# Turning k, q and v by VectorE blocks and DRAM in the mixer, and decays from running sums

## The chip, the cores and the metric

The kernel runs on one core of a Trainium2 chip. Its time is device microseconds of one execution; three runs are shown for the kernel before. Beside them stands one profiled execution, from which all durations below come. PE is TensorE, DVE is VectorE, ACT is ScalarE, POOL is GpSimd, and SP is the engine that issues most of the DMAs.

## The reference

One layer of a hybrid decoder trunk in float32, with 256 positions and a width of 2048:

```python
h = rmsnorm(x, norm_mix_w)
q, k, v, z, b_raw, a_raw, p_in, g_a, g_b = split(h @ w_in)
q, k, v = split(silu(causal_dwconv(concat(q, k, v), conv_qkv_w)))     # 4 taps along the sequence
q, k = l2norm per head (16 heads of 128); beta = sigmoid(b_raw)
g = -exp(a_log) * softplus(a_raw + dt_bias)                            # log decay per position and head
# gated delta rule in chunks of 64: cumsum of g in the chunk, decay[i, j] = exp(g_i - g_j) for j <= i,
# a unit lower triangular solve, attention inside the chunk, a state carried from chunk to chunk
y_a = rmsnorm(o) * silu(z)
y_b = (trailing means of p_in - p_in) @ pool_w * pool_scale
x = x + (sigmoid(g_a) * y_a + sigmoid(g_b) * y_b) @ w_out
h = rmsnorm(x, norm_ffn_w); gate, up = split(h @ w_up)
x = x + (gelu(causal_dwconv(gate) + bias) * up) @ w_down
return rmsnorm(x)
```

## The kernel before

**Weights.** Every weight matrix is streamed once, in chunks of 256 rows by 512 columns (512 KB, `raw`, four buffers, loaded by SP in L110). ACT rounds a chunk to the fast fp32 format (`whi`, L112), DVE makes the rest (`wlo`, L119); both have three buffers. PE then does three products in place of one (L149, L150, L151): 12 matmuls of 128x512 for a chunk. Chunks are begun two ahead of the one in use (`AHEAD`).

**Stages.** The mixer works through four groups g of four heads. Each group is a row of gemms: k, q, v, the pooling's input, the gate g_b, the pooling's own product, z and the gate g_a, nearly all of eight chunks. The output projection, the FFN (22 gemms of eight chunks) and the last projection follow. The output projection is begun before group 3 of the mixer is finished.

**Work beside the gemms.** A gemm's result lies in PSUM with positions on the partitions. `evict` (ACT, L422) copies it out. The convolution wants channels on the partitions, so `conv_silu` (L425) calls `turned` (L167), which has PE transpose the 128x128 blocks into PSUM (L175): eight for each of k, q and v. ACT starts the convolution (L436), DVE adds three taps (L439), and the tanh form of silu ends in `kq` or `vT` (L443). The list `later` holds such work until the second chunk of the following gemm. The solve of a group, `gdn` (L445), is a generator, advanced once for each half chunk (`side`). It first makes the decays: DVE scales a triangular matrix by the log decays in two parts (r0, r1; L464, L465), PE sums them with `lowr` and `onesr` (L472, L473, L475), ACT exponentiates (L476, L477, L480), POOL clears the part above the diagonal (L482). Later it has PE turn v back to positions on partitions (L553), and ACT scales that into `vt` (L555).

In the FFN the same need is met by `flip` (L155): DVE transposes all 32x32 blocks of an evicted tile in one instruction (L158), four DMAs write the blocks to their places in DRAM (L162), and one reads the turned tile back (L164).

**Order.** A scheduler places each engine's instructions in one fixed sequence when the kernel is built; on the chip each engine takes them strictly in that order and waits on semaphores. DMAs are queued on the engine that issues them, nearly all on SP.

## Time and profile before

| | us |
|---|---|
| runs, median (lowest to highest) | 1582.16 (1582.14 to 1584.18) |
| profiled execution | 1581.35 |
| its span on the core | 1579.6 |
| PE busy | 1556.7 (99% of the span) |
| DVE busy | 1040.2 (66%) |
| ACT busy | 745.8 (47%) |
| POOL busy | 89.4 (6%) |
| mean granted clock | 0.997 |

The span is what the profiler saw on the core; the time is measured around it. A row of a group names line, engine, operation, tiles (written <- read), shapes and count, then busy time and mean ns of one, then the idle time just before with what ended it. A row of waits names who waited at which line for whom, then total us, number and longest. A row of the stage table gives the window, its length, PE's busy time and count, the granted clock, DMA's share and GB/s. A timeline row gives start and duration in us, then engine, line and operation. DMAs are listed with KB each and median us from issue to landing. Matmuls overlap, so their durations add up to more than their share of time.

### The profile page before, as it was taken

To read this page: it belongs to the slowest core of one execution; us is meant where nothing else is said; L and a number is where in the kernel's file an instruction comes from. 1 tells how busy PE (TensorE), PEld (TensorE's weight loads), DVE (VectorE), ACT (ScalarE), POOL (GpSimd) and SP (SyncE) were. 2 spreads that over 40 slices of the span, in tenths; PEclk is the share of its full clock that TensorE was granted. 3 is DMA by queue.
4 is the path that set the end of the run, shared out by engine and by line. 5 is a ranking of instruction groups with operands and counts; after the bars stand their busy time and mean duration, and the time that the engine had idled before them with its cause. 6 is when DMAs were issued, how large, how long until landed. Compare 5 with 4: busy or idle time off the path is not lost.

```text
span 1579.6 us, 20017 instructions
## 1 busy us (share of the span) xinstructions
PE 1556.7 (99%) x7408; PEld 1284.3 (81%) x7408; DVE 1040.2 (66%) x1544; ACT 745.8 (47%) x925; POOL 89.4 (6%) x121
## 2 busy tenths in 40 slices
PE   8999999999999999999999999999999999999997
PEld 6878888888888888787888888888788878888885
DVE  5778757786678757795655666665666666444445
ACT  6545436444545435454454455444454445434344
POOL 3020100100010100102000000000000000000000
PEclk9999999999999999999999999999999999999998
DMA  7656656665556655565555878788777787755553
GB/s 253 181 155 195 193 148 173 167 197 173 155 153 190 197 149 175 164 191 176 198 188 187 238 224 243 242 244 247 232 234 251 230 246 234 239 196 191 196 191 132
DMA packets 263736, 314.61 MB, mean 199 GB/s; under 512 B 109894, under 2 KB 124246, under 8 KB 263510
## 3 DMA queue, kind: packets, MB, share of 16 engines
q1 hardware_dynamic: 260928, 308.85, 64.5%
q10 hardware_dynamic: 2710, 4.48, 0.8%
q8 instruction: 58, 0.95, 0.2%
q14 instruction: 40, 0.33, 0.1%
HBM read 298.61 MB, written 14.68 MB: 198 GB/s over the span
## 4 chain that ended last, share of the span: by engine, by line
PE 86%; DMA 4%; DVE 4%; issue 3%; SPq 1%; POOL 1%; ACT 0%; DVEq 0%; POOLq 0%
PE psm L151 22%; PE psm L150 21%; PE psm L149 21%; PE psg L840 3%; PE psm L839 3%; PE psg L839 2%; PE psm L838 2%; PE psg L838 2%; PE psm L840 2%; DVE wlo L119 2%; DMA gs<-flip 1%; SPq L162 1%; PE psg L491 1%; DMA flip<-tn 1%; PE psg L175 1%
## 5 line engine op out<-in xcount | busy, mean ns | idle before, releaser
L119 DVE TENSOR_TENSOR wlo<-raw,whi 128x1024 fp32r<-128x1024 f32 x528 | 648.5, 1233 | 376.1 <-ACT whi L112 368.6
L112 ACT CAST whi<-raw 128x1024 fp32r<-128x1024 f32 x530 | 556.9, 1053 | 716.2 <-PE psm L150 548.2
L151 PE MATMUL psm<-wlo,xhl 128*128 128x512 f32 x896 | 353.1, 394 | 2.1 <-DVE wlo L119 2.1
L149 PE MATMUL psm<-whi,xhl 128*128 128x512 f32 x896 | 352.3, 393 | 1.3 <-ACT xhl L219 1.3
L150 PE MATMUL psm<-whi,xhl 128*128 128x512 f32 x896 | 351.9, 393 | 0.0
L151 PE MATMUL psm<-wlo,fhl 128*128 128x512 f32 x704 | 273.7, 390 | 1.9 <-DVE wlo L119 1.4
L150 PE MATMUL psm<-whi,fhl 128*128 128x512 f32 x704 | 274.0, 389 | 0.0
L149 PE MATMUL psm<-whi,fhl 128*128 128x512 f32 x704 | 273.9, 389 | 0.0
L151 PEld LDWEIGHTS psm<-wlo,xhl 128*128 128x128 f32 x896 | 168.6, 188 | 37.8 <-DVE wlo L119 3.7
L149 PEld LDWEIGHTS psm<-whi,xhl 128*128 128x128 f32 x896 | 168.7, 188 | 35.4 <-ACT xhl L219 1.7
L150 PEld LDWEIGHTS psm<-whi,xhl 128*128 128x128 f32 x896 | 168.7, 188 | 34.7
L151 PEld LDWEIGHTS psm<-wlo,fhl 128*128 128x128 f32 x704 | 132.1, 188 | 32.0 <-DVE wlo L119 4.8
L150 PEld LDWEIGHTS psm<-whi,fhl 128*128 128x128 f32 x704 | 132.2, 188 | 27.6
L149 PEld LDWEIGHTS psm<-whi,fhl 128*128 128x128 f32 x704 | 132.2, 188 | 27.1
L838 PE MATMUL psg<-whi,hhi 128*128 128x512 f32 x176 | 68.5, 389 | 0.0
L838 PE MATMUL psm<-whi,hhi 128*128 128x512 f32 x176 | 68.5, 389 | 0.0
L839 PE MATMUL psm<-whi,hlo 128*128 128x512 f32 x176 | 68.5, 389 | 0.0
L839 PE MATMUL psg<-whi,hlo 128*128 128x512 f32 x176 | 68.5, 389 | 0.0
L840 PE MATMUL psm<-wlo,hhi 128*128 128x512 f32 x176 | 68.5, 389 | 0.0
L840 PE MATMUL psg<-wlo,hhi 128*128 128x512 f32 x176 | 61.1, 389 | 0.0
L439 DVE SCALAR_TENSOR_TENSOR cy<-psg,cqw,cy 128x255 f32<-128x255 f32 (+1 forms) x144 | 60.5, 473 | 0.4 <-ACT cy L436 0.4
L151 PE MATMUL psm<-wlo,mhi 128*128 128x512 f32 x128 | 50.0, 391 | 0.3 <-DVE wlo L119 0.3
(223 smaller groups left out, 1351.7 us busy)
## 6 DMA issues: line engine op xcount, KB each, us to landing
raw<-in_w_in_dram SPq DMA_DIRECT2D x226, 512.0 KB, 3.9
raw<-in_w_up_dram SPq DMA_DIRECT2D x176, 512.0 KB, 4.5
raw<-in_w_down_dram SPq DMA_DIRECT2D x88, 512.0 KB, 4.5
raw<-in_w_out_dram SPq DMA_DIRECT2D x32, 512.0 KB, 3.5
flip<-tn SPq DMA_DIRECT2D x88, 128.0 KB, 4.7
gs<-flip SPq DMA_DIRECT2D x22, 512.0 KB, 4.7
raw<-in_pool_w_dram SPq DMA_DIRECT2D x8, 512.0 KB, 4.1
x<-in_x_dram SPq DMA_DIRECT2D x4, 512.0 KB, 6.9
```

The source lines that it names most:

```text
L112: nc.scalar.copy(hi, raw)
L119: nc.vector.tensor_tensor(lo, raw, hi.bitcast(F32), op=ALU.subtract)
L149: mm(ps[:, t, :], lh(k, t), hi[:, kk, :], start=(k == 0), stop=False)
L150: mm(ps[:, t, :], ll(k, t), hi[:, kk, :], start=False, stop=False)
L151: mm(ps[:, t, :], lh(k, t), lo[:, kk, :], start=False, stop=(k == nk - 1))
L162: nc.sync.dma_start(dv[a], b[32 * a : 32 * a + 32].rearrange("p t (f j) -> p t f j", j=32))
L175: nc.tensor.transpose(pt[:, ff, t * P : (t + 1) * P], src[:, t, f * P : (f + 1) * P], ident)
L439: nc.vector.scalar_tensor_tensor(y[:, f, s:], gs[:, : S - s], w(j), y[:, f, s:], op0=ALU.mult, op1=ALU.add)
L491: mm(pg0, kq[:, h, 0, 0:P], kq[:, h, :, :], start=True, stop=True)
L838: mm(acc[c][t], lh(k, t), hi[:, kk, :], start=(k == 0), stop=False)
L839: mm(acc[c][t], ll(k, t), hi[:, kk, :], start=False, stop=False)
L840: mm(acc[c][t], lh(k, t), lo[:, kk, :], start=False, stop=(k == KF - 1))
```

## The change

- The evicted k, q and v go through `flip` (with its target as an argument now) instead of PE, straight into `kq` and `vT`; `conv_silu` reads them from there. Its DVE transpose writes into the convolution's own buffers (tag cy).
- After silu, v goes back through a new `flip_back`: one DVE transpose, four DMAs to DRAM, one back into `vt`, where ACT scales it in place.
- The decays no longer use scaled triangles. Once, PE makes running sums of the log decays in each chunk, written to DRAM as rows (`rund`), and six shifts for each position and head. For a group the rows are read back, broadcast to all partitions; POOL puts -1e30 above the diagonal, and ACT takes 24 exponentials of 128x64, each with its shift as bias.

In the diff below, lines in plain words stand for longer pieces that are only removed or are small set-up.

```diff
-    def flip(pool, src, tag, bufs):
-        b = pool.tile([P, 2, 512], F32, tag="tn", name=nm("tn"))
+    def flip(pool, tag, bufs, src, dst):
+        b = pool.tile([P, 2, 512], F32, tag=tag, bufs=bufs, name=nm("tn"))
         nc.vector.transpose(b.rearrange("p t f -> p (t f)"), src.rearrange("p t f -> p (t f)"))
         d = dpool.tile([512, S], F32, tag="flip", name=nm("flip"))
         dv = d.rearrange("(f i) (t a j) -> a i t f j", i=32, t=2, j=32)
         for a in range(4):
             nc.sync.dma_start(dv[a], b[32 * a : 32 * a + 32].rearrange("p t (f j) -> p t f j", j=32))
-        o = pool.tile([P, 4, S], F32, tag=tag, bufs=bufs, name=nm(tag))
-        nc.sync.dma_start(o, d.rearrange("(f p) s -> p f s", p=P))
-        return o
+        nc.sync.dma_start(dst, d.rearrange("(f p) s -> p f s", p=P))
+
+    def flip_back(pool, tag, bufs, src, dst):
+        b = pool.tile([P, 4, S], F32, tag=tag, bufs=bufs, name=nm("tb"))
+        nc.vector.transpose(b.rearrange("p h s -> p (h s)"), src.rearrange("p h s -> p (h s)"))
+        d = dpool.tile([S, 512], F32, tag="back", name=nm("back"))
+        dv = d.rearrange("(n i) (h a j) -> a i h n j", i=32, h=4, j=32)
+        for a in range(4):
+            nc.sync.dma_start(dv[a], b[32 * a : 32 * a + 32].rearrange("p h (n j) -> p h n j", j=32))
+        nc.sync.dma_start(dst.rearrange("p t h d -> p t (h d)"), d.rearrange("(t p) c -> p t c", p=P))
...
+    nc.gpsimd.memset(tri[0:64, 64:P], 0.0)
...
-    onesr, lowr, ghi, glo, tail
+    ntri, ntail, top
...
+    psr = pg([NH, S])
+    for t in range(2):
+        mm(psr[:, t * P : (t + 1) * P], glog[:, t, :], tri, start=True, stop=True)
+    runs = mp.tile([NH, S], F32, name="runs")
+    nc.vector.tensor_copy(runs, psr)
+    rund = dpool.tile([NH, S], F32, tag="rund", bufs=1, name="rund")
+    nc.sync.dma_start(rund, runs)
+    pse = pg([P, 6, NH])
+    for n, mat in ((0, ntri), (2, ntail)):
+        mm(pse[:, n : n + 2, :], mat, glog, start=True, stop=True)
+    mm(pse[:, 4, :], low, glog[:, 0, :], start=True, stop=True)
+    mm(pse[:, 5, :], low, glog[:, 0, :], start=True, stop=False)
+    mm(pse[:, 5, :], top, glog[:, 1, :], start=False, stop=True)
+    shift = mp.tile([P, 6, NH], F32, name="shift")
+    nc.vector.tensor_copy(shift, pse)
...
-    def conv_silu(e, kind, g, dst):
-        pts = turned(e)
+    def conv_silu(kind, g, dst):
...
-            gs = pts[f // 2][:, f % 2, :]
+            gs = dst[:, f, :]
...
-    (gdn: per pair of heads 8 scalings of tri, 6 matmuls, 4 exponentials from PSUM, 2 selects)
+        nc.sync.dma_start(dec0, rund[4 * g : 4 * g + 4, :].partition_broadcast(P))
+        yield
+        for d, src in ((dec1, dec0[:, :, P:S]), (dec0[:, :, 0:P], dec0[:, :, 0:P])):
+            nc.gpsimd.affine_select(d, src, pattern=[[0, 4], [1, P]], compare_op=ALU.is_ge, fill=-1e30, base=0,
+                                    channel_multiplier=-1)
+        yield
+        for h in range(4):
+            hh = 4 * g + h
+            for d, n in ((dec0[:, h, 0:64], 0), (dec0[:, h, 64:P], 2), (dec0[:, h, P : P + 64], 4),
+                         (dec0[:, h, P + 64 : S], 5), (dec1[:, h, 0:64], 1), (dec1[:, h, 64:P], 3)):
+                nc.scalar.activation(d, d, AF.Exp, bias=shift[:, n, hh : hh + 1])
+            if h % 2:
+                yield
...
         for h in range(4):
             yield
-            pvt = pg([P, 2, P])
             for t in range(2):
-                nc.tensor.transpose(pvt[:, t, :], vT[:, h, t * P : (t + 1) * P], ident)
-            for t in range(2):
-                nc.scalar.activation(vt[:, t, h, :], pvt[:, t, :], AF.Copy, scale=nk[:, t, h : h + 1])
+                nc.scalar.activation(vt[:, t, h, :], vt[:, t, h, :], AF.Copy, scale=nk[:, t, h : h + 1])
...
             ps = ps_k0 if kind == 1 and g == 0 else gemm_a(xh, xl, KD)
-            e = evict(ps)
-            later.append(lambda e=e, kind=kind, g=g, dst=dst: conv_silu(e, kind, g, dst))
+            flip(mp, "cy", 2, evict(ps), dst)
+            later.append(lambda kind=kind, g=g, dst=dst: conv_silu(kind, g, dst))
+            if kind == 2:
+                later.append(lambda vT=vT, vt=vt: flip_back(mp, "cy", 2, vT, vt))
...
```

The kernel has 85 more DMAs, all on SP: five for each of 12 turns and four turns back, four broadcasts and one write. The scheduler gives new orders. Three places follow; in the rows "waits" names the semaphores (DMAHW a DMA's), and numbers behind a name tell buffers apart.

ACT, group 1, from q's convolution on, where decays are made. Before (L436 convolution, L476, L477 and L480 exponentials, L442 tanh, L112 casts):

```order
L436 ACTIVATE cy_385_2306<-psg_383_2296,cqw_338 128x256 [waits PE_49]
L436 ACTIVATE cy_385_2306<-psg_384_2301,cqw_338 128x256 [waits PE_49]
L476 ACTIVATE dec0_396_2344<-psg_402_2364 128x2x128 [waits PE_49]
L477 ACTIVATE dec1_397_2345<-psg_404_2366 128x256 [waits PE_49]
L112 CAST whi_416_2426<-raw_415_2424 128x1024 [waits DMAHW1_49,DVE_49,PE_49]
L436 ACTIVATE cy_385_2306<-psg_383_2296,cqw_338 128x256 [waits DVE_49]
L436 ACTIVATE cy_385_2306<-psg_384_2301,cqw_338 128x256 [waits DVE_49]
L112 CAST whi_425_2458<-raw_424_2456 128x1024 [waits DMAHW2_49,PE_49,Activation_49]
L480 ACTIVATE dec0_396_2344<-psg_403_2365,tail_490 128x128 [waits PE_49]
L480 ACTIVATE dec0_396_2344<-psg_403_2365,tail_490 128x128
L476 ACTIVATE dec0_396_2344<-psg_412_2409 128x2x128 [waits PE_49]
L112 CAST whi_428_2484<-raw_427_2482 128x1024 [waits DMAHW3_49,PE_49,Activation_49]
```

The changed kernel there:

```order
L112 CAST whi_374_2304<-raw_373_2302 128x1024 [waits DMAHW2_49,DVE_49,PE_49]
L477 ACTIVATE dec0_381_2319<-dec0_381_2319,shift_502 128x64 [waits DMAHW4_49,DVE_49,Pool_49]
L477 ACTIVATE dec0_381_2319<-dec0_381_2319,shift_502 128x64
L477 ACTIVATE dec1_382_2320<-dec1_382_2320,shift_502 128x64 x2
L477 ACTIVATE dec0_381_2319<-dec0_381_2319,shift_502 128x64 x2
L477 ACTIVATE dec1_382_2320<-dec1_382_2320,shift_502 128x64 x2
L477 ACTIVATE dec0_381_2319<-dec0_381_2319,shift_502 128x64 x2
L477 ACTIVATE dec1_382_2320<-dec1_382_2320,shift_502 128x64
L477 ACTIVATE dec0_381_2319<-dec0_381_2319,shift_502 128x64 [waits Pool_49]
L477 ACTIVATE dec0_381_2319<-dec0_381_2319,shift_502 128x64 x5
L112 CAST whi_384_2336<-raw_383_2334 128x1024 [waits DMAHW3_49,DVE_49,PE_49]
L477 ACTIVATE dec1_382_2320<-dec1_382_2320,shift_502 128x64
```

The exponentials of a group now come in two long bursts between casts and wait for the rows' DMA and for POOL, not for PE; the convolution comes later.

ACT, group 1, after v's convolution. Before (L555 scales v, turned back by PE, into `vt`; L689 rounds the pooling's tile, L422 evicts):

```order
L112 CAST whi_493_2882<-raw_492_2880 128x1024 [waits DMAHW0_49,PE_49]
L112 CAST whi_497_2905<-raw_496_2903 128x1024 [waits DMAHW5_49,PE_49,Activation_49]
L112 CAST whi_503_2931<-raw_502_2929 128x1024 [waits DMAHW6_49,DVE_49,PE_49]
L555 ACTIVATE vt_392_2340<-psg_480_2827,nk_394_2342 128x128 [waits PE_49,Pool_49]
L555 ACTIVATE vt_392_2340<-psg_480_2827,nk_394_2342 128x128
L555 ACTIVATE vt_392_2340<-psg_488_2850,nk_394_2342 128x128 [waits PE_49]
L555 ACTIVATE vt_392_2340<-psg_488_2850,nk_394_2342 128x128
L555 ACTIVATE vt_392_2340<-psg_489_2861,nk_394_2342 128x128 [waits PE_49,Pool_49]
L555 ACTIVATE vt_392_2340<-psg_489_2861,nk_394_2342 128x128
L689 CAST phi_482_2835<-psg_490_2866 128x512 [waits PE_49]
L112 CAST whi_512_2999<-raw_511_2997 128x1024 [waits DMAHW7_49,DVE_49,PE_49]
L689 CAST phi_482_2835<-psg_491_2873 128x512 [waits PE_49]
```

The changed kernel (L436 evicts, L684 rounds the pooling's tile, L547 scales `vt`):

```order
L112 CAST whi_449_2760<-raw_448_2758 128x1024 [waits DMAHW3_49,PE_49]
L112 CAST whi_458_2795<-raw_457_2793 128x1024 [waits DMAHW4_49,PE_49,Activation_49]
L436 ACTIVATE ev_453_2787<-psm_420_2540,rs_51_371 128x512 [waits PE_49]
L436 ACTIVATE ev_453_2787<-psm_420_2540,rs_51_371 128x512
L112 CAST whi_463_2831<-raw_462_2829 128x1024 [waits DMAHW5_49,DVE_49,PE_49]
L112 CAST whi_466_2851<-raw_465_2849 128x1024 [waits DMAHW6_49,DVE_49,PE_49]
L684 CAST phi_454_2790<-psg_460_2815 128x512 [waits PE_49]
L547 ACTIVATE vt_306_1916<-vt_306_1916,nk_379_2317 128x128 [waits DMAHW5_49,Pool_49]
L547 ACTIVATE vt_306_1916<-vt_306_1916,nk_379_2317 128x128 x3
L547 ACTIVATE vt_306_1916<-vt_306_1916,nk_379_2317 128x128 [waits Pool_49]
L547 ACTIVATE vt_306_1916<-vt_306_1916,nk_379_2317 128x128 x3
L684 CAST phi_454_2790<-psg_461_2822 128x512 [waits PE_49]
```

The eight scalings wait for the DMA that brings v back, and they stand between the two halves of the pooling's tile, with the cast behind them.

SP, the gemms of k and q of group 1. Before, there are only weight loads (L110); now the turn (L162 to DRAM, L163 back) and the decays' broadcast (L467) stand among them:

```order
L110 DMA raw_349_2162<-in_w_in_dram 128x2x512 [waits DMAHW3_49,DVE_49]
L110 DMA raw_352_2180<-in_w_in_dram 128x2x512 [waits DMAHW4_49,DVE_49]
L162 DMA flip_336_2081<-tn_335_2079 64x16x32 [waits DVE_49]
L162 DMA flip_336_2081<-tn_335_2079 64x16x32 x3
L110 DMA raw_355_2198<-in_w_in_dram 128x2x512 [waits DMAHW5_49,DVE_49]
L110 DMA raw_358_2216<-in_w_in_dram 128x2x512 [waits DMAHW6_49,DVE_49]
L110 DMA raw_361_2234<-in_w_in_dram 128x2x512 [waits DMAHW7_49,DVE_49]
L163 DMA kq_304_1914<-flip_336_2081 128x4x256 [waits DMAHW2_49,DMAHW3_49,DMAHW1_49,DMAHW4_49,DMAHW0_49,PE_49]
L110 DMA raw_368_2264<-in_w_in_dram 128x2x512 [waits DVE_49]
L110 DMA raw_373_2302<-in_w_in_dram 128x2x512 [waits DMAHW5_49,DVE_49]
L110 DMA raw_383_2334<-in_w_in_dram 128x2x512 [waits DMAHW6_49,DVE_49]
```

The load of `kq` waits for PE as well, which has to be done with the group before; the weight loads behind it wait with it.

At the end of the mixer PE has 24 matmuls of the output projection between group 3's last product of the solve (L628) and the transposes of the gated result (L183); before there were 44 between L636 and L175.

More of the change, by code (lines that the diff above doesn't have):

```diff
@@ L291 @@
     nc.vector.tensor_scalar(rsq, rs1, 0.25, None, op0=ALU.mult)
+    low = mp.tile([P, P], F32, name="low")
+    nc.gpsimd.affine_select(low, ones, pattern=[[-1, P]], compare_op=ALU.is_gt, fill=0.0, base=0,
+                            channel_multiplier=1)
     tri = mp.tile([P, P], F32, name="tri")
@@ L296 @@
                             channel_multiplier=-1)
-    low = mp.tile([P, P], F32, name="low")
-    nc.gpsimd.affine_select(low, ones, pattern=[[-1, P]], compare_op=ALU.is_gt, fill=0.0, base=0,
-                            channel_multiplier=1)
-    onesr = mp.tile([P, P], F32R, name="onesr")
-    nc.vector.tensor_copy(onesr, ones)
-    lowr = mp.tile([P, P], F32R, name="lowr")
-    nc.vector.tensor_copy(lowr, low)
+    nc.gpsimd.memset(tri[0:64, 64:P], 0.0)
+    ntri = mp.tile([P, P], F32, name="ntri")
+    nc.gpsimd.tensor_scalar(ntri, tri, -1.0, None, op0=ALU.mult)
+    ntail = mp.tile([P, P], F32, name="ntail")
+    nc.gpsimd.tensor_copy(ntail, ntri)
+    nc.gpsimd.tensor_copy(ntail[0:64, 0:64], low[0:64, 0:64])
+    top = mp.tile([P, P], F32, name="top")
+    nc.gpsimd.memset(top, 0.0)
+    nc.gpsimd.memset(top[0:64], 1.0)
     def same_block(b, name, tag):
@@ L662 @@
         vT = mp.tile([P, 4, S], F32, tag="vT", bufs=1, name=nm("vT"))
+        vt = mp.tile([P, 2, 4, P], F32, tag="vt", name=nm("vt"))
         for kind, dst in ((1, kq[:, :, 0, :]), (0, kq[:, :, 1, :]), (2, vT)):
@@ L788, in features @@
             nc.scalar.activation(e[:, t, :], ps[:, t, :], AF.Copy, scale=rs2[:, t : t + 1])
-        return flip(fp, e, "gs", 2)
+        o = fp.tile([P, 4, S], F32, tag="gs", bufs=2, name=nm("gs"))
+        flip(fp, "tn", 1, e, o)
+        return o
     hhi = []
```

46 lines of the change are left out of this document (4 added, 42 removed).

## The prediction

> **What bounds the kernel now.** I read the page first (busy times, the chain), then PE's waits, then the stage table, then timelines at the places that the change edits.
>
> ```profile
> span 1579.6 us, 20017 instructions
> PE 1556.7 (99%) x7408; PEld 1284.3 (81%) x7408; DVE 1040.2 (66%) x1544; ACT 745.8 (47%) x925; POOL 89.4 (6%) x121
> PE 86%; DMA 4%; DVE 4%; issue 3%; SPq 1%; POOL 1%; ACT 0%; DVEq 0%; POOLq 0%
> PE psg L206 <- DMA nmrows<-in_norm_mix_w_dram: 4.6, 1, 4.6
> PE psm L151 <- DVE wlo L119: 3.7, 8, 0.9
> 100.00:745.00 645.00, 642.21 (x3322) 1.00 0.60 174
> 846.00:1330.00 484.00, 482.12 (x2124) 1.00 0.78 235
> ```
>
> PE is busy 99% of the span and 86% of the chain; after the start it waits for weights for 3.7 us in all. In the mixer (100 to 745 us, which the change edits) PE idles 645.00 − 642.21 = 2.8 us, in the FFN (846 to 1330) 1.9 us; the granted clock is 1.00 in both. So a PE instruction removed from the mixer is worth its full spacing, and every wait that the change adds is worth its length, less what the prepared weights cover.
>
> That cover is read from the steady rows in the FFN, where each chunk of 12 matmuls needs a cast (whi, ACT) and a subtraction (wlo, DVE):
>
> ```profile
> 1092.31 1.05 ACT L112 CAST whi<-raw 128x1024 fp32r<-128x1024 f32 x1 [1.66 <-PE psm L150]
> 1093.40 1.23 DVE L119 TENSOR_TENSOR wlo<-raw,whi 128x1024 fp32r<-128x1024 f32 x1 [1.50 <-ACT whi L112]
> 1095.03 1.05 ACT L112 CAST whi<-raw 128x1024 fp32r<-128x1024 f32 x1 [1.67 <-PE psm L150]
> ```
>
> A cast starts when PE frees a buffer, three chunks back, and one follows another by 2.72 us. The chunk that needs it starts two chunks (5.44 us) later: the cast (1.05) has 4.4 us to spare. The subtraction ends 2.32 us after the cast's start and is first read two matmuls into the chunk, so it has 5.44 + 0.45 − 2.32 = 3.6 us. ACT idles 1.66 us in each chunk, DVE 1.50. A wait of ACT or DVE ahead of these two reaches PE only beyond 3.6 us.
>
> **What PE loses.**
>
> ```profile
> L175 PE MATMUL psg<-ident,ev 128*128 128x128 f32 x96 | 12.8, 272 | 0.0
> L553 PE MATMUL psg<-ident,vT 128*128 128x128 f32 x32 | 4.8, 272 | 0.0
> L472 PE MATMUL psg<-r,lowr 128*128 128x256 f32 x16 | 4.6, 297 | 0.0
> 292.10 1.03 PE L175 MATMUL psg<-ident,ev 128*128 128x128 f32 x8
> 292.89 0.48 PE L151 MATMUL psm<-wlo,xhl 128*128 128x512 f32 x1
> 293.20 0.39 PE L149 MATMUL psm<-whi,xhl 128*128 128x512 f32 x1
> 86.61 0.28 PE L472 MATMUL psg<-r,lowr 128*128 128x256 f32 x1
> 86.73 0.40 PE L150 MATMUL psm<-whi,xhl 128*128 128x512 f32 x1
> 86.97 0.28 PE L472 MATMUL psg<-r,lowr 128*128 128x256 f32 x1
> ```
>
> Durations overlap, so I count by starts. From 292.10 to 293.20 lie eight transposes and one matmul; a chunk is 12 matmuls in 2.72 us, 0.227 each, so the eight cost 0.87 us, 0.109 each. A decay matmul moves the next start by 86.73 − 86.61 = 0.12. Gone are 96 transposes of k, q, v (10.4 us), the 32 of v back (L553, 3.5 us) and 48 decay matmuls (L472, L473, L475: 5.8 us). Added are seven matmuls for running sums and shifts, once; as plain fp32 each shows as two records, so 14 by at most 0.12, 1.7 us, 0.2 of it in place of the old tail's. The balance is −18.2 us, all of it on the path to the end, since PE hardly idles there.
>
> **What the turn costs elsewhere.** The FFN already does 22 such turns. One of them:
>
> ```profile
> L158 DVE STREAM_TRANSPOSE tn<-fev 128x1024 f32<-128x1024 f32 x22 | 27.3, 1243 | 0.0
> 1089.12 1.25 DVE L158 STREAM_TRANSPOSE tn<-fev 128x1024 f32<-128x1024 f32 x1
> 1090.39 5.01 SPq L162 DMA_DIRECT2D flip<-tn  x4
> 1097.98 0.37 SPq L164 DMA_DIRECT2D gs<-flip  x1
> 1103.79 0.41 DVE L797 TENSOR_SCALAR y<-gs,cfw,vec 128x256 f32<-128x256 f32 x1 [3.73 <-DMA gs<-flip]
> DVE y L797 <- DMA gs<-flip: 23.1, 11, 3.7
> DVE y L806 <- DMA gs<-flip: 31.3, 11, 3.6
> gs<-flip SPq DMA_DIRECT2D x22, 512.0 KB, 4.7
> flip<-tn SPq DMA_DIRECT2D x88, 128.0 KB, 4.7
> raw<-in_w_in_dram SPq DMA_DIRECT2D x226, 512.0 KB, 3.9
> ```
>
> From the transpose's start to the first use are 14.7 us here; a turn whose waits are all at their shortest (transpose 1.25, two transfers of 4.7, issues of 1.3) would take 12. DVE waits 54 us for the 22, up to 3.7 each, and PE loses at most its 1.9 us: 0.09 per turn, because four casts and subtractions stand between transpose and use, and four chunks (10.9 us) plus 3.6 to spare hold 14.5.
>
> DVE's own work stays about even (16 transposes of 1.24 us come, 64 scalings of tri, L464 and L465, go). ACT gets 24 exponentials of 128x64 a group for 8 larger ones. No row has that shape, so I bound one by these:
>
> ```profile
> L362 ACT ACTIVATE uu<-na 128x32 f32<-128x32 f32 x1 | 0.2, 219 | 0.0
> L480 ACT ACTIVATE dec<-psg,tail 128x128 f32<-128x128 f32 x16 | 5.0, 363 | 0.0
> 310.82 1.66 ACT L555 ACTIVATE vt<-psg,nk 128x128 f32<-128x128 f32 x6
> ```
>
> Between 219 and 363 ns; nearest by size is the first, and I take 250: 24 are 6.0 us (5.3 to 8.7), to be fitted into idle time of 1.66 a chunk. That is off PE's path by itself and matters where it meets a wait.
>
> The new waits, place by place in the new order; each is reckoned by hand with a landing of 12 us, and the range has 14.7:
> - **k of groups 1 to 3.** Only three subtractions stand between transpose and use. SP's load of the turned tile also has to wait until PE has read the old q for its norm (L633), in the q gemm's third chunk, and three weight loads and the decays' broadcast are queued behind it on SP. From that read on PE has about 9.0 us of prepared work; load 4.7, the four scalings and the subtraction behind eight convolution steps take 10.4. 1.4 each, I take 1.5: 4.5 us.
> - **q of groups 1 to 3.** DVE reaches the transpose 5.5 us after the gemm's end, behind the last multiplications of the group before, instead of the 2.1 of an FFN turn; and two bursts of exponentials stand between the casts. 1.7 each: 5 us.
> - **v, four times**: an FFN turn, 0.3 each: 1 us.
> - **v back, four times.** ACT's eight scalings of vt (0.27 each by the six in 1.66, 2.2 us) wait for the DMA, and every cast behind waits with them. From the tanh's end: 1.3 us to the transpose, 12 of landing, 2.2 of scalings and 0.6 for the pooling's copy give 16.1; the next cast is due 11.5 after it: 4.6 to 6 late (one subtraction can stand in between), less 3.6: 1.0 to 2.4. Between the transpose itself and the scalings stand only three casts. I take the upper end, 2.3 each, since DVE is busier here than in the FFN: 9 us.
> - **Group 0's decays.** Running sums to DRAM (one transfer), broadcast back (another), two selects on POOL, 24 exponentials, all between two casts, and started behind q's convolution: 5 us (0 if the sums are early, 8 by the 14.7).
> - **End of the mixer.** Today the last norm is covered:
>
> ```profile
> 766.31 0.60 ACT L646 ACTIVATE o<-psg 128x512 f32<-128x512 f32 x1 [2.98 <-PE psg L636]
> 767.90 1.64 POOL L651 TENSOR_TENSOR ro<-ro,epsx 128x8 f32<-128x8 f32 x1 [43.41 <-DVE ro L650]
> 774.13 1.23 DVE L717 TENSOR_TENSOR sz<-sz,yb 128x1024 f32<-128x1024 f32 x1
> 776.13 1.03 PE L175 MATMUL psg<-ident,sz 128*128 128x128 f32 x8
> ```
>
>   From 766.31 to 775.36 are 9.0 us, and PE has 44 matmuls (10.0 us) ahead of the transposes. In the new order group 3's solve ends some seven chunks later, and 24 matmuls (5.4 us) are left: 9.0 − 5.4 = 3.6, less a subtraction that moves out of the chain in part: 3 us.
>
> Together 27.5 us. The same hand reckoning gives 0.4 us for an FFN turn where the rows have 0.09, so I take 0.25 off each of 16 turns: 23.5. Of the mixer's 2.8 us of old idle time I let 2 go, since the old places are gone.
>
> Sum: 1581.35 (the profiled execution: span 1579.6 and 1.75 around it) − 18.2 − 2 + 23.5 = 1584.65; the median of the runs shown is 0.8 above the profiled one, so **1585**.
>
> One rule speaks against the change. The Trainium skill (VectorE: DVE Perf Modes, The three transpose paths) gives a 128x128 transpose to TensorE when PSUM is an acceptable target, and says that a plain DMA whose strides do the transposing is 19 times slower than the crossbar's. The trace agrees with the first half in the latency (0.109 us against 12 to 14.7 for a turn) and not with the second here: a turn's transfers (4.7 and 4.7) are 2.4 plain loads of 3.9, because VectorE has turned within the 32x32 blocks already. A second page (DMA: Bandwidth & Descriptors, Specifications) wants at least 512 B a transfer for the line rate; pieces here are 128 B. By that rule DMA would be the bound, and that is the last rival below.
>
> **The rivals.**
> - *Hidden as in the FFN* (faster). If the landing is 12 us or less where four casts stand between, the turns cost 0.09 each (1.4 us), the group-0 chain 1.5 and the end 3: 1582.2 − 20.2 + 6 = 1568. For it: 22 turns in the FFN at 78% DMA share lose nothing, and the mixer's share is 0.60. Against: DVE and ACT are fuller in the mixer, k has three casts between, and vt's scalings stand on ACT itself. It decides at 20.2 us of new waits, 1.3 per turn if they all were equal.
> - *The scalings hold the casts* (slower). With landings of 14.7 everywhere, each of the 11 turns that I have at the edge (k and q of groups 1 to 3, v back, group 0's q) costs 2.7 − 1.6 = 1.1 us more: 1585 + 12 = 1597.
> - *DMA the bound.* If the two transfers of a turn (9.4 us) stopped the weight loads for that long, the two chunks loaded ahead (5.44) would leave 4.0 on each of 16: 1582 − 20 + 63 = 1625. The FFN's 0.09 speaks against it.
> - *The change does not pay on PE*: transposes that PE did while it waited anyway. 2.8 us of idle time in 645 leave no room; not given a chance of its own.
>
> **How the numbers follow.** Hidden 0.35, my sum 0.42, held casts 0.20, DMA 0.03. What can be told from no change is 0.2%, 3.2 us: 1579.0 to 1585.3. My sum's own range is 1578 to 1592 (±7 from the landing on 11 turns at 0.25 to 1.1 and the two single chains), about half of it within the bound. So faster 0.35 + 0.02, same 0.20 + 0.01, slower the rest, 0.42. The range of 8 in 10 goes from the hidden case to the held casts: 1568 to 1597.
>
> **What would show it.** PE: groups with ident,ev and ident,vT gone, and the mixer's PE busy time shorter by 18 us; if it is shorter by 10, the transposes were not 0.109. PE's waits: rows of psm L149 for whi and L151 for wlo of 15 us or more together; under 8 is the hidden case. ACT's waits: vt L547 for the back transfer 4 times at 4 us or more, cy L449 12 times at 2 to 4; if L547 shows under 3 my 9 us fall. The transposes of sz at the mixer's end should wait about 3 us for DVE L712. The prediction is wrong above all if the new tiles land in less than 12 us, or if ACT waits in these places without PE following.

## The result, and the profile after

The changed kernel takes 1605.09 us (median of 4 runs, 1601.17 to 1606.44) against 1583.17 beside it: a ratio of 1.0134, 95% interval 1.0119 to 1.0149. That is 22 us slower, beyond the forecast of 1585 and beyond the upper end of its range, 1597. The profiled run took 1604.47.

The heads of the page and of the chain, PE's longer waits, and the two stages (length, PE busy, instructions, granted clock, DMA share, GB/s):

```profile
span 1602.8 us, 19814 instructions
PE 1557.4 (97%) x7244; PEld 1270.6 (79%) x7244; DVE 1047.2 (65%) x1493; ACT 760.0 (47%) x989; POOL 96.2 (6%) x119
PE 55%; DMA 5%; DVE 3%; SPq 2%; ACT 1%; issue 1%; POOL 1%; POOLq 0%; DVEq 0%; ACTq 0%
...
PE psm L151 <- DVE wlo L119: 7.7, 16, 1.0
PE psm L149 <- ACT whi L112: 7.6, 6, 1.8
PE psg L572 <- POOL T L557: 5.5, 5, 1.8
PE psg L486 <- DVE kq L456: 5.1, 1, 5.1
...
100.00:745.00 645.00, 630.44 (x3068) 0.99 0.71 198
866.00:1353.00 487.00, 484.44 (x2124) 1.00 0.78 234
```

PE executes 164 instructions fewer, and yet its busy time is 1557.4 against 1556.7. Its idle time between 100 and 745 us rose from 2.8 to 14.6 us, and the granted clock there fell to 0.99. So two things ate the gain: waits, and a slower clock, which makes what is left of the work longer. The transposes and the decay matmuls are gone as intended, and the waits in the new places are there, behind the transfers that the prediction named:

```profile
ACT dec L477 <- POOL dec L470: 16.1, 4, 4.9
ACT vt L547 <- DMA vt<-back: 13.6, 4, 5.2
ACT cy L449 <- DMA kq<-flip: 13.3, 7, 3.6
ACT cy L449 <- DMA vT<-flip: 6.3, 4, 2.5
```

**Where 23 us are.** Durations of matmuls overlap, so I reckon by starts, as the prediction did. Both kernels have the same 6,335 matmuls against prepared weights; whatever one takes up to the next start beyond 0.227 us is lost. That loss went from 19.2 to 52.0 us (+32.8). All other PE work went from 106.7 to 96.9 (−9.8). The sum, +23.0, agrees with the spans (+23.2). The parts, from the starts at each place of the trace after:

| part | us |
|---|---|
| PE work removed | −17.5 |
| wait before group 0's first gram (decays) | +5.3 |
| turn back of v, four groups (2.4, 0.3, 2.7, 0.6) | +6.0 |
| q and the decays of groups 1 to 3 (1.35, 2.05, 2.3) | +5.7 |
| k of groups 1 to 3 | +1.8 |
| end of the mixer | +2.8 |
| longer waits at the starts of the triangular solves | +4.8 |
| half clock (7.7 on these matmuls, about 2.9 on other work) | +10.6 |
| FFN and after | +2.9 |

These make 22.4; the rest is in small gaps. A row gives the whole gaps of the trace after; the gaps of the trace before (2.8 us in the mixer) are not taken off.

**The half clock.** One place shows how a wait becomes a clock loss: group 2's v. First ACT and SP, then PE's records, in order of start:

```profile
500.70 0.37 SPq L173 DMA_DIRECT2D vt<-back  x1
...
506.91 2.45 ACT L547 ACTIVATE vt<-vt,nk 128x128 f32<-128x128 f32 x8 [4.35 <-DMA vt<-back]
509.27 0.56 ACT L684 CAST phi<-psg 128x512 fp32r<-128x512 f32 x1
509.73 2.94 ACT L112 CAST whi<-raw 128x1024 fp32r<-128x1024 f32 x3
```

```profile
508.63 0.39 PE L151 MATMUL psm<-wlo,xhl 128*128 128x512 f32 x1
510.83 0.50 PE L149 MATMUL psm<-whi,xhl 128*128 128x512 f32 x1 [1.81 <-ACT whi L112]
511.16 0.40 PE L150 MATMUL psm<-whi,xhl 128*128 128x512 f32 x1
512.09 0.50 PE L151 MATMUL psm<-wlo,xhl 128*128 128x512 f32 x1 [0.53 <-DVE wlo L119]
512.42 0.39 PE L149 MATMUL psm<-whi,xhl 128*128 128x512 f32 x1
512.66 0.54 PE L150 MATMUL psm<-whi,xhl 128*128 128x512 f32 x1
512.99 0.63 PE L151 MATMUL psm<-wlo,xhl 128*128 128x512 f32 x1
513.42 0.63 PE L149 MATMUL psm<-whi,xhl 128*128 128x512 f32 x1
```

ACT waits 4.35 us for the turned tile, scales, copies for the pooling, and only then casts: PE is 1.81 us late. That was forecast. What was not: from 512.99 on the matmuls start 0.43 us apart instead of 0.227, for the next 3.4 us, though nothing waits any more. Pairs of neighbouring stretches of 3.4 us, after (columns as in the stage rows above):

```profile
137.30:140.70 3.40, 1.31 (x5) 1.00 0.44 113
140.70:144.10 3.40, 3.40 (x8) 0.50 0.81 208
...
451.30:454.70 3.40, 1.68 (x6) 1.00 0.96 202
454.70:458.10 3.40, 3.40 (x9) 0.50 0.85 286
639.10:642.50 3.40, 1.67 (x7) 0.99 0.83 203
642.50:645.90 3.40, 3.40 (x9) 0.50 0.83 302
```

In each pair PE was busy for less than half of the first stretch, and the second is granted half the clock. The stretches lie on a fixed grid of 3.41 us. Where the limit lies, the traces don't say sharply. Pairs from three experiments that come below (no_back, prefetch, dec_wide):

```profile
555.80:559.20 3.40, 1.79 (x28) 1.00 0.83 264
559.20:562.60 3.40, 3.40 (x10) 0.51 0.59 174
```

```profile
698.40:701.80 3.40, 1.63 (x7) 1.00 0.15 24
701.80:705.20 3.40, 3.40 (x17) 1.00 0.80 264
```

```profile
358.90:362.30 3.40, 2.06 (x38) 0.99 0.80 236
362.30:365.70 3.40, 3.40 (x10) 0.50 0.69 214
```

1.79 busy (0.527) is followed by half the clock, 1.63 (0.472 of its grid stretch) is not, and 2.06 (0.609) is. Over all 19 traces, in the stretches of the grid at full clock up to 30 us before the end, all 23 with a busy share under 0.47 are followed by half the clock; from 0.47 to 0.61 some are and some are not; none above 0.61 is. So the busy share of these records is a good sign of the half clock, but no sharp threshold. Such a stretch costs about 1.7 us where PE has work throughout. Before had none until its end; after has six at 92.9 (6.8 us long), 140.7, 454.7, 512.7, 642.5 and 758.5: 23.9 us at half rate. The Trainium skill (TensorE: Matmul & The Clock Gate, What's actually happening) describes a free-running window of 3413 ns and a clock set by how busy PE has been; the traces agree, for every change of the granted clock lies on that grid. The Trainium skill's section Why this matters for your kernels, on the same page, warns of idle gaps over about 3 us; here a gap of 1.81 us with a second of 0.53 in the same stretch was enough, and the measurement decides.

### The profile page after: what moved, and what is told of

It is laid out like the page before. It is cut to its first block, busy times and chain, and to the rows that moved or that the text cites. A ratio compares the mean times of both kernels' runs of the same rounds, so it can differ in the third digit from the quotient of the medians.

```text
span 1602.8 us, 19814 instructions
## 1 busy us (share of the span) xinstructions
PE 1557.4 (97%) x7244; PEld 1270.6 (79%) x7244; DVE 1047.2 (65%) x1493; ACT 760.0 (47%) x989; POOL 96.2 (6%) x119
## 4 chain that ended last, share of the span: by engine, by line
PE 55%; DMA 5%; DVE 3%; SPq 2%; ACT 1%; issue 1%; POOL 1%; POOLq 0%; DVEq 0%; ACTq 0%
PE psm L151 13%; PE psm L149 13%; PE psm L150 12%; PE psg L835 2%; PE psg L836 2%; PE psg L837 2%; PE psm L837 2%; PE psm L835 2%; PE psm L836 2%; DMA gs<-flip 2%; DVE wlo L119 1%; SPq L162 1%; DMA flip<-tn 1%; DVE y L798 1%; POOL T L557 1%
## 5 line engine op out<-in xcount | busy, mean ns | idle before, releaser
L119 DVE TENSOR_TENSOR wlo<-raw,whi 128x1024 fp32r<-128x1024 f32 x528 | 657.4, 1252 | 376.0 <-ACT whi L112 374.2
L112 ACT CAST whi<-raw 128x1024 fp32r<-128x1024 f32 x530 | 555.5, 1053 | 680.8 <-PE psm L150 477.0
L149 PE MATMUL psm<-whi,mhi 128*128 128x512 f32 x128 | 50.8, 397 | 1.8 <-ACT whi L112 1.8
```

What stands on the lines that cost most here:

```text
L112: nc.scalar.copy(hi, raw)
L119: nc.vector.tensor_tensor(lo, raw, hi.bitcast(F32), op=ALU.subtract)
L149: mm(ps[:, t, :], lh(k, t), hi[:, kk, :], start=(k == 0), stop=False)
```

## The experiments

The theory after the first look: the waits of the decays and of the turn back of v, which make PE late by 2 us and bring on the half clock, carry the loss, and the turns of k, q and v are nearly covered. The rival: the DMA engines are the bound, since their share in the mixer rose from 0.60 to 0.71 and a weight load takes 4.3 us instead of 3.9.

**One half each.** After, with the decays made by PE as before; and before, with the new decays.

```diff
 # turns_only: after, and
-    nc.sync.dma_start(dec0, rund[...].partition_broadcast(P)) ...
+    r0, r1 = tri * glog ...; mm(pd0, lowr, r0 ...) ...
 # decays_only: before, and the opposite edit
```

> The turns of k, q, v and v back as in the changed kernel, the decays by PE as before. Theory A (new waits of PE in single places, and 3.4 us of half clock after each stretch of 3.4 us in which PE stood still for over half): the two places of group 0's decays go (5.5 us of wait before the first gram, and two of the seven half-clock stretches, 1.7 us each), the waits at the back turn, at the solve's start and at the mixer's end stay. PE's gain is 13.9 us instead of 18.2. 1605 - 5.5 - 3.4 + 4.3 = about 1600, between 1595 and 1602; four or five half-clock stretches. Theory B (the turns' small DMA pieces slow all of PE's and DVE's work, wherever it is): all 16 turns are there, so 1605 + 4.3 less the broadcasts' share, 1606 to 1609.

> The decays from running sums as in the changed kernel, all turns by PE as before. Theory A: PE gains 4.3 us; group 0's chain (rows to DRAM, back, select, 24 exponentials, tanh, gram) costs up to 5.5 us of wait and one or two half-clock stretches (1.7 to 3.4), the bursts in the other groups 0 to 1 each: 1583 - 4.3 + 5.5 + 3.4 + 1 = 1588, between 1582 and 1590. Theory B: no small pieces in DMA, so 1583 - 4.3 = 1579, no half clock.

turns_only: 1585.94, ratio 1.0023 (1.0014 to 1.0033): +3.7 us. decays_only: 1596.09, 1.0089 (1.0068 to 1.011): +13.9. Both expectations missed, turns_only far below its range of 1595 to 1602 and decays_only above its 1582 to 1590. The decays carry most of the loss, and 22 is 4 to 5 more than the two apart; with the intervals as they are, this excess is not clear of noise. What happens to decays_only in group 0:

```profile
74.62 1.23 POOL L464 TENSOR_SCALAR_AFFINE_SELECT dec<-dec 128x512 f32<-128x512 f32 x2 [50.43 <-DMA dec<-rund]
...
75.30 4.41 ACT L471 ACTIVATE dec<-dec,shift 128x64 f32<-128x64 f32 x18 [1.43 <-POOL dec L464]
...
82.71 2.94 ACT L112 CAST whi<-raw 128x1024 fp32r<-128x1024 f32 x3
83.80 0.50 PE L149 MATMUL psm<-whi,xhl 128*128 128x512 f32 x1 [2.13 <-ACT whi L112]
```

18 exponentials in 4.41 us are 0.245 each, as estimated (0.25). But they don't trickle into the idle time of ACT: they stand in one burst ahead of the convolution, the tanh and the next cast, which comes 7.4 us after the burst's start.

**Without the turn back; with its scalings on POOL.**

```diff
 # no_back: after, and
-    nc.scalar.activation(vt[:, t, h, :], vt[:, t, h, :], AF.Copy, scale=nk[...])
+    nc.tensor.transpose(pvt[:, t, :], vT[:, h, t * P : (t + 1) * P], ident)
+    nc.scalar.activation(vt[:, t, h, :], pvt[:, t, :], AF.Copy, scale=nk[...])
-    later.append(lambda vT=vT, vt=vt: flip_back(mp, "cy", 2, vT, vt))
 # vt_pool: after, and
-    nc.scalar.activation(vt[...], vt[...], AF.Copy, scale=nk[...])
+    nc.gpsimd.tensor_scalar(vt[...], vt[...], nk[...], None, op0=ALU.mult)
```

> The changed kernel, but v goes back by PE (32 transposes) as before. Theory A: PE pays 3.5 us again, ACT's scalings no longer wait for a DMA: about 6 us of waits of PE and two or three half-clock stretches (3.4 to 5.1) go: 1605 + 3.5 - 10 = 1598, between 1595 and 1601. Theory B: 4 of 16 turns go: a quarter of the 40 us that were lost against the sum of PE's gain, so 1605 + 3.5 - 10 = 1598 as well, but with no half-clock stretch less. The half-clock stretches tell them apart.

> The changed kernel, but the eight scalings of vt in each group are done by POOL, which nobody's weights wait for, instead of ACT. All turns and all DMAs stay. Theory A: ACT's casts are not held at the back turn any more: 1605 less 6 us of waits and less two or three half-clock stretches: 1594 to 1599. Theory B: same DMAs, same loss: 1605.

no_back: 1596.78, 1.0094 (1.0071 to 1.0117): the turn back, beside the new decays, costs 6 to 8 us, although it saves PE 3.5. Of the six stretches of half clock three are left, as theory A of its expectation had it. vt_pool: 1600.31, 1.011 (1.0093 to 1.0127): 4 to 5 of these come back when the scalings leave ACT, with the same transfers; it misses its 1594 to 1599, and its interval overlaps that of after a little. That speaks against DMA as the bound, and so does a row that is the same before and after: ACT's casts wait 0.2 us in all for the mixer's weight loads.

**What of the decays costs?** Three kernels: after, with the exponentials held until q is finished (a shift that depends on q), so that they stand behind the tanh; decays_only with three wide exponentials for the 24 small ones, leaving out the shifts; decays_only with the rows from a constant tile, leaving out the broadcast from DRAM. The last two do not compute the layer's decays.

```diff
 # dec_after_q: after, and
+    nc.vector.scalar_tensor_tensor(shq, <kq, 0 * its value>, 0.0, shift[:, :, 4 * g : 4 * g + 4], ...)
-    nc.scalar.activation(d, d, AF.Exp, bias=shift[:, n, hh : hh + 1])
+    nc.scalar.activation(d, d, AF.Exp, bias=shq[:, n, h : h + 1])
 # dec_wide: decays_only, and
-    (24 of) nc.scalar.activation(d, d, AF.Exp, bias=shift[...])
+    (3 of) nc.scalar.activation(d, d, AF.Exp)
 # dec_local: decays_only, and
-    nc.sync.dma_start(dec0, rund[...].partition_broadcast(P))
+    (selects read the constant tile cneg instead of dec0)
```

> The changed kernel with the exponentials of a group made to depend on the finished q (their shifts get zero times an element of q added, by one small DVE instruction a group), so that they come behind the tanh of q's convolution and no longer ahead of it; same DMAs, same selects, same 24 exponentials. Theory A (ACT's fixed order: the burst, waiting for POOL's select, holds the tanh and the casts): group 0's 5.1 us before the first gram and its two half-clock stretches (3.4) go, and part of the 5.7 us and of the half clock at the same place in groups 1 to 3: 1605 - 8 - 4 = 1593, between 1588 and 1598. Rival (the longer chain through DRAM itself costs the time): 1602 to 1606.

> The kernel with only the decays changed, but with three exponentials of 128x512 a group without shift in place of 24 of 128x64 with theirs (the decays' values are wrong so). Theory A (burst): ACT is held for 1.8 us instead of 6, the gaps before group 0's gram and at the same place later shrink by about 1 us each, half-clock stretches fall away: 1596 - 4 to 8 = 1588 to 1592. Rival (chain through DRAM and POOL): the wait for the select stays, 1594 to 1597.

> The kernel with only the decays changed, with the rows taken from a constant tile in place of the broadcast from DRAM (the values are wrong so; one select more a group), the 24 exponentials as they are. Theory A (burst): 24 exponentials still stand ahead of the tanh, but can start earlier, since nothing waits for DMA: 1590 to 1596. Rival (chain): 1596 less 5 us of group 0 and up to 1 in each other group: 1586 to 1589.

dec_after_q: 1596.0, 1.008 (1.0054 to 1.0106), 9 us less than after with the same transfers and the same exponentials; its row of the wait before the first gram is gone, and so is ACT's wait for POOL's selects. The place of the exponentials matters here, with their number the same. This is the second run that speaks against the DMA rival. dec_wide: 1586.05, 1.0025 (1.0012 to 1.0038), 10 less than decays_only. dec_local: 1585.34, 1.0008 (0.9995 to 1.0022), 11 less, though all 24 small exponentials are still there. Here neither theory that these two were to part stands alone: both times lie under theory A's range. PE's waits for whi and wlo in the mixer (from 20 us to the FFN's first matmul) are 2.3 us before, 3.4 in dec_wide, 3.2 in dec_local and 9.2 in decays_only. So a burst without the late chain adds about 1 us of them, and so does the late chain without the burst. Neither kernel is free for all that: PE has 4.3 us less to do in both and they are no faster than before, since 4.6 us of waits for the solve's T remain (0.7 before; more on these below), and in dec_wide two stretches of half clock. ACT's waits for the selects and what reached PE in dec_local, where in decays_only they were 9.2, 4, 2.8 for the first, and 4.0 us in 5 waits for whi:

```profile
ACT dec L474 <- POOL dec L467: 4.7, 5, 1.5
...
PE psm L151 <- DVE wlo L119: 4.8, 8, 1.6
PE psm L149 <- ACT whi L112: 0.9, 1, 0.9
```

My reading: a cast has 4.4 us to spare, one burst takes 4.4, one late select 2 to 5, so either fits and both don't. The scheduler's order differs in each of these kernels too, and that was not held fixed.

**k, q and v alone, with two repairs.** k, q and v turned, v back and decays on PE; then four more chunks of the output projection ahead of the mixer's end; then two more half chunks between the solve's loads and their first use; and that last edit in turns_only.

```diff
 # kqv_only: turns_only with the edit of no_back
 # kqv_early: kqv_only, and
-    early = [gemm_a(at(mhi), at(mlo), KD, range(n)) for n in (6, 2)]
+    early = [gemm_a(at(mhi), at(mlo), KD, range(n)) for n in (6, 6)]
 # kqv_wait: kqv_early, turns_wait: turns_only, and
-        for _ in range(WAIT):
+        for _ in range(WAIT + 2):
```

> Only k, q and v turned by VectorE and DRAM; v back by PE and the decays by PE as before. Theory A: against the kernel with all turns (1586) PE pays 3.5 us again and the waits at the back turn go (1.0, 1.2, 1.7 and 1.9 us by its gaps): 1586 + 3.5 - 5.8 = 1583.5, between 1581 and 1585, no difference from before. Theory B (the loss goes by the number of turns): 12 of 16 of the 17.6 us lost there, less 10.4: 1585.

> As the kernel with only k, q and v turned, and four more chunks of the output projection begun before the mixer's last group is finished (six and six instead of six and two). Theory A: the idle time at the mixer's end (about 1.1 + 0.7 + 1.1 us in the kernel with all turns) is covered: 3 us less than without, 1580 or 1581. Rival: those gaps come from casts that are late for another reason, and nothing changes.

> As the kernel with k, q and v turned and six and six early chunks, with two half chunks more between the loads of the solve's blocks (lb) and their first use on DVE. Theory A: in that kernel DVE waits 4 to 5 us for these loads, which the turns have made later, with a subtraction behind; PE's gaps there (0.5, 0.6, 1.3 and 1.3 us) go: 1587 - 3 = 1584. Rival: the scheduler fills the place with other work and the wait turns up at the next use, 1587.

> All turns, v back too, decays by PE, with two half chunks more between the solve's loads and their use. Theory A: 1586 less the 3.6 us that the same step gave without the back turn, as far as the gaps at that place (1.2, 1.7 and 1.9 us) are the loads' and not the back turn's: 1582 to 1584. Rival (these gaps are the back turn's, where ACT's scalings wait): 1585 to 1587.

kqv_only: 1586.34, 1.0023 (1.0005 to 1.0041), a little above its 1581 to 1585 and no different from turns_only: beside the old decays the turn back costs nothing that shows. kqv_early: 1587.43, 1.003 (1.0018 to 1.0043): the end's wait was no loss that more prepared work repairs; my expectation of 1580 to 1581 was wrong. kqv_wait: 1583.83, 1.0006 (0.9994 to 1.0018), equal to before and the best version here, but not better. turns_wait: 1586.91, 1.0024 (1.001 to 1.0038), no gain. The wait that kqv_wait was to shorten, in kqv_only:

```profile
681.83 0.42 DVE L544 TENSOR_TENSOR tmp<-lb,tb 128x248 f32<-128x248 f32 x1 [5.31 <-DMA lb<-cdd]
682.28 0.42 DVE L546 TENSOR_TENSOR tb<-tb,tmp 128x248 f32<-128x248 f32 x1
682.62 1.22 DVE L119 TENSOR_TENSOR wlo<-raw,whi 128x1024 fp32r<-128x1024 f32 x1
...
683.89 0.75 PE L151 MATMUL psm<-wlo,xhl 128*128 128x512 f32 x1 [1.89 <-DVE wlo L119]
684.44 0.63 PE L149 MATMUL psm<-whi,xhl 128*128 128x512 f32 x1
```

A subtraction stands behind DVE's wait for the solve's loads, PE is 1.89 us late, and the half clock follows. kqv_wait has no stretch of half clock in the mixer; but DVE still waits 13.7 us there for these loads (18.1 in kqv_only), and the same step gave turns_wait nothing, so how much of its gain comes from the step stays open.

**A wait set by hand (failed).** To measure the half clock by itself, before with weight buffers left unused at chosen chunks, so that PE would wait long in one kernel and twice as often but shortly in the other.

```diff
 # gaps_long: before, and (gaps_short: the same with tag "wlo" at chunks 3 and 6)
+    SKIP = {UP + 8 * m + c for m in range(4, 16) for c in (5,)}
+    for _ in range(2 if len(made) in SKIP else 0):
+        wpool.tile(shape, F32R, tag="whi", name=nm("skip"))
```

> The kernel before, with the cast of one chunk in each of 12 FFN gemms made to wait for the chunk just ahead (two buffers of whi skipped): in 12 places PE waits about 1.3 us for the cast and 0.9 for the subtraction, 26 us in all. Theory A (a 3.4 us window of which PE was idle over half is followed by 3.4 us of half clock): most of the 12 places, say 6 to 10, bring one, 1.7 us each: 1582 + 26 + 10 to 17 = 1618 to 1625, and the granted clock shows it. Theory B (half clock comes only after PE has stood still for a whole window of 3.4 us): 1582 + 26 = 1608, clock as before.

> The kernel before, with the subtraction of two chunks in each of the same 12 gemms made to wait for the chunk just ahead (two buffers of wlo skipped): 24 places where PE waits 0.9 to 1.0 us, 22 to 24 us in all, nearly as much as in the other kernel with gaps but cut into halves. Theory A: no window is idle for over half, so no half clock: 1582 + 23 = 1605. Theory B: the same 1605. A theory in which the loss goes by the sum of idle time would give it as many half-clock stretches as the long gaps, 1615 to 1622.

1582.98, 1.0006 (0.9989 to 1.0022) and 1583.09, 1.0002 (0.999 to 1.0014). The waits never arose (PE waits for wlo 3.8 and 4.5 us in all, 3.7 before), so nothing was tested: a tile that nothing uses held no buffer here. The rule of the half clock above is therefore read from traces, not produced at will.

**Decays a group ahead (failed).** If place matters, decays that are made a group before they are used, in tiles of their own, should cost nothing.

```diff
 # dec_prefetch: decays_only, and (prefetch: kqv_wait with the new decays, and)
-    nc.sync.dma_start(dec0, ...); selects and exponentials in gdn's steps
+    later.append(decays)   # the same instructions, ahead of gdn; dec0, dec1 handed in
-    on = mp.tile([P, 2, 4, P], F32, tag="dec0", name=nm("on"))
+    on = mp.tile([P, 2, 4, P], F32, tag="T", name=nm("on"))   # and o2 in a tile of its own
 # dec_prefetch_same: dec_prefetch, and
+    for _ in range(4):
+        yield              # four empty half chunks at gdn's head
 # prefetch_same: prefetch without kqv_early's and kqv_wait's edits, with the four yields
```

> The kernel with only the decays changed, but each group's rows are fetched and its exponentials taken at the start of the group's code, in tiles of their own, so that the scheduler places those of groups 1 to 3 in the quiet stretch of the group before (the solve becomes four half chunks shorter with it). Same instructions, same transfers. Theory A (place in the order): what groups 1 to 3 lose goes; PE's gain of 4.3 us stays against group 0's 3 us and one half-clock stretch: 1582 to 1585, where the parent had 1596. Rival (the 24 exponentials and the broadcasts cost wherever they stand): 1592 to 1596.

> As the kernel before last with k, q and v turned (1584: v back by PE, six and six early chunks, two half chunks more for the solve's loads), with the decays from running sums made a group ahead. Theory A: 1584 - 4.3 of PE's work + 1 to 4 for group 0 = 1581 to 1584. Rival: the decays cost 13 as they did alone: 1592 to 1597.

> The kernel with only the decays changed and taken a group ahead, with four empty half chunks at the head of the solve, so that the solve stands where it does when the decays are made in it. Theory A (place in the order; the solve's shift made the last one slow): the gaps at the solve's loads fall from 10.7 us to about the 4.2 of the kernel without the step, those at q's place stay away: 1601 - 6.5 = 1594 or a little less, below the 1596 of the kernel without the step, 1590 to 1595. Rival (the new place itself costs): 1599 to 1602.

> k, q and v turned, v back by PE, decays a group ahead, with the four half chunks back in the solve and without the other two steps (early chunks, later use of the loads). Theory A: the kernel with the same turns and the decays in the solve took 1597; the gaps at q's place of groups 1 to 3 (1.5, 1.3 and 1.9 us) go: 1592, between 1590 and 1595. Rival (the new place itself costs): 1599 to 1604.

1601.28, 1.0111 (1.0092 to 1.013); 1603.23, 1.0117 (1.0092 to 1.0142); 1599.37, 1.0105 (1.0086 to 1.0124); 1600.8, 1.0096 (1.0065 to 1.0127). None is better than decays_only's 1596.09; the first two lie above the ranges of both theories, the last two in that of their rivals. In dec_prefetch the gaps at q's place in groups 1 to 3 are gone, but those at the solve's loads grew from about 4.2 to 10.7 us in all. DVE's wait for these loads, in before, dec_prefetch, prefetch, and the two with the old spacing (decays_only has 14.6 and kqv_wait 13.7, in four waits each):

```profile
DVE tmp L538 <- DMA lb<-cdd: 12.1, 4, 3.4
```

```profile
DVE tmp L512 <- DMA lb<-cdd: 18.2, 4, 5.4
```

```profile
DVE tmp L518 <- DMA lb<-cdd: 33.0, 4, 9.1
```

```profile
DVE tmp L514 <- DMA lb<-cdd: 18.1, 4, 5.5
```

```profile
DVE tmp L520 <- DMA lb<-cdd: 30.8, 4, 9.0
```

I had put the growth down to the solve starting four half chunks sooner, and this fell: with the old spacing the rows stay. The place that was meant was not tested: the exponentials of groups 1 to 3 did not land in a quiet stretch but run in dec_prefetch from 125.4, 304.8 and 491.5 us, beside DVE's waits for the loads of the solve ahead (ended at 132.4, 311.3 and 498.3). Those three waits are 4.6, 5.1 and 5.4 us, and the fourth, which has no exponentials beside it, 3.1. This points to the exponentials' new place rather than to `on`, which now shares its buffer with the solve's tiles in every group; neither was tried alone.

## Why the prediction was wrong

The direction with the largest chance, slower, was right; the size was not, and the 1585 itself still lay within what the prediction counted as no change. By the steps:

- **PE's work removed**: −18.2 forecast, −17.5 by starts. Right.
- **The new places in sum**: 23.5 forecast; the table's 5.3 + 6.0 + 5.7 + 1.8 + 2.8 is 21.6. Right in sum. Singly: group 0's decays 5.3 (5), q and decays 5.7 (5), the end 2.8 (3); the turn back 6.0 (9) and k 1.8 (4.5) were sized too high. The end is right by luck: the prediction had the transposes of sz wait for DVE, and what PE waited for there are two casts and a subtraction (0.91, 0.53 and 0.91 us by their rows).
- **No term for the clock: the step that failed.** I read 1.00 for both stages of before and took it for a constant. The sum holds waits alone; 10.6 us of half clock came with them. The prediction had the two numbers that mattered, waits of about 2 us and a clock in the profile's rows, and before shows no stretch in its steady part from which the link could be read.
- **"The old places are gone", −2 us, and no term for the solves: the second step that failed.** PE's wait for the solve's T (L572 now, L580 before) did not go, it grew from 0.7 to 5.5 us, and by starts the solves' heads lose 4.8 more. I had costed them at nothing. Together with the 2 us this is 6.8 of the miss. The wait before, and what stands beside T on DVE, before and after:

```profile
PE psg L580 <- POOL T L565: 0.7, 1, 0.7
```

```profile
181.73 2.54 POOL L565 TENSOR_TENSOR T<-tcm,eb 128x512 f32<-128x512 f32 x2
181.80 2.55 DVE L465 TENSOR_SCALAR r<-tri,glo 128x128 fp32r<-128x128 f32 x2 [1.19 <-POOL TT L565]
```

```profile
195.37 4.55 DVE L119 TENSOR_TENSOR wlo<-raw,whi 128x1024 fp32r<-128x1024 f32 x2
196.57 4.48 POOL L557 TENSOR_TENSOR T<-tcm,eb 128x512 f32<-128x512 f32 x2
```

  Before, in groups 0 to 2, the next group's scalings of tri stood beside T, and one T took 1.28 us. The new decays remove these scalings, DVE's subtraction for wlo moves up beside T, and both get slow: T 2.26, the subtraction 2.27 instead of 1.22. T is slow like this in the other groups of after, in group 3 of before, and in the kernels with the new decays (mean 2.0 to 2.3 in all eleven, 1.5 in the eight with the old). So "DVE's own work stays about even" was right by the sum and missed what the removed work had kept apart. This is read from the traces; no run puts the scalings back alone.
- **The FFN**: nothing forecast, +2.9 in the two profiled runs. From its first matmul to its last it takes 721.8 to 726.4 us in all 19 traces, 722.8 before and 725.7 after, and 723.9 and 725.5 in the two kernels that turned out like before. So these 2.9 are within the scatter of one profile and no effect of the change.

10.6 + 6.8 + 2.9 − 1.9 (places) + 0.7 (work) are 19.1 of the 19.9 us by which the spans miss the forecast's +3.3.

The rivals: "hidden as in the FFN" fell for the change as a whole (new waits of 21.6 us where it allowed 6), and comes nearest with k, q and v alone and two more edits (kqv_wait, 1.0006). "The scalings hold the casts" had the right mechanism, but landings of 14.7 us would have given 1597; vt_pool shows 4 to 5 us of it. "DMA the bound" does not stand against dec_after_q and vt_pool, 9 and 4 to 5 us faster with the same transfers, and ACT's 0.2 us of waits for the mixer's weights. The prediction also held a turn's two transfers against a factor of 19 by comparing them with plain loads; that factor is against a crossbar transfer, which no run here uses, so the trace doesn't decide it. The signs that I set: whi and wlo waits of 15 us or more (15.3: met); vt behind the back transfer 4 times (13.6 in all, so 3.4 in the mean, under the 4 that I named: my 9 us fell to 6); cy L449 12 times at 2 to 4 (11 times, 1.8 in the mean); PE 18 us less busy in the mixer (1.4 less from 20 us to the FFN's first matmul, 822.79 to 821.42, above all since half clock lengthens what is left); sz behind DVE at the end (not seen).

## What to carry to other kernels

Where TensorE is the bound and its clock is full, price a new wait twice: its own length, and half a window of clock if waits leave PE busy for less than about half of a 3.4 us window; one wait of 1.8 us with a short second one did that. Work that "fits into idle time" fits only if it is spread; ask in what order a burst and a late arrival stand before the next cast, for each alone added about 1 us of waits for the weights and the two together 7. Ask also what the work that you remove has kept apart: without the scalings, a subtraction came beside POOL's product and both slowed. Taking 17 us off the bound engine paid nothing here: new waits in the queues on which PE's weights depend (21.6 us), longer waits at the solves and the half clock took more than that back.

## What the runs showed of the hardware

- The clock: in 19 traces every window of the 3.41 us grid at full clock with PE busy under 0.47 was followed by one at half the clock (matmuls 0.43 us apart instead of 0.227); between 0.47 and 0.61 it went either way.
- POOL's product of 128x512 took 1.28 us beside DVE's scalings and 2.26 beside DVE's subtraction of 128x1024, which then took 2.27 instead of 1.22.
- A wait's row is shorter than its cost: at 508.63 a matmul of 0.39 starts, the next could have started at 508.86 and starts at 510.83, 1.97 later, while the row says 1.81. With some 28 waits the rows fall 4 to 5 us short.
- A turn of a 128x1024 tile through DRAM, written in pieces of 128 bytes, kept its price in the mixer at a DMA share of 0.71 (flip<-tn 4.4, kq<-flip 4.5, vT<-flip 4.9 us; 4.7 and 4.7 in the FFN before).
